# GpSimd subtracts the last contraction tile of a weight's low part

## The chip, the cores and the metric

The kernel runs on one core of one Trainium2 chip. The metric is the device time of one execution in microseconds (us), the median of several runs. Before the change it is 1791.72 us (three runs, 1791.2 to 1794.84).

## The reference

One decoder layer on a sequence of 256 tokens with 2048 channels, all in fp32. A conditioning vector `c` is turned into six vectors by a 2048 x 12288 matrix (`w_ada`): shift, scale and gate for each of two sub-layers. Then:

```
h = x * (1 + sc1) + sh1
proj = h @ w_in                      # 2048 x 13344: q, k, v of two mixers, z, b, a, two gates
y_a  = softmax attention, 8 heads of 128, relative-position bias (256 tokens are one block)
y_b  = gated DeltaNet, 16 heads of 128: short conv, l2 norm of q and k, chunked delta rule, gated RMS norm
y    = (sigmoid(gate_a) * (y_a @ w_proj_moba) + sigmoid(gate_b) * (y_b @ w_proj_gdn)) @ w_out
x    = layer_norm(alpha * x + g1 * y)
h    = x * (1 + sc2) + sh2
y    = (silu(gate) * up) @ w_ffn_out,  gate, up = split(h @ w_ffn_in)     # 2048 x 11264, 5632 x 2048
out  = layer_norm(alpha * x + g2 * y)
```

## The kernel before, in words

**Three products for one.** TensorE multiplies in fp32r, a rounded fp32. For accuracy each fp32 operand is split into a high part (the value rounded to fp32r) and a low part (the value minus its high part), and a product is taken as high x high + high x low + low x high. The activations are split once. Each weight is split as it comes in.

**One load of a weight.** `load_w` (L196) brings one block of a weight from HBM into a buffer `raw` of 128 partitions x 1024 elements at most; the block holds `kn` contraction tiles of 128 rows, `cn` columns each, side by side. `split_w` (L202) makes the parts: ScalarE copies `raw` to `hi` (L206), which rounds it, and VectorE subtracts, `lo = raw - hi` (L207). `raw`, `hi` and `lo` have four buffers each. The loads are issued by SP (SyncE) in one queue, in order; the load that reuses a buffer waits until the readers of the old contents are done.

**The list of steps.** `step` (L250) appends to a list a pair: the load with its split, and the matmuls that use it. `run(3)` walks the list and calls load and split up to three steps ahead of the matmuls. A scheduler then orders each engine's instructions by this order and its own estimate of when each can start; on the chip each engine works through its own queue in order, and semaphores tie the engines together. GpSimd's queue holds, besides a little arithmetic, the issue of some 70 small DMAs (`sdma`), which store and reload intermediate results through HBM.

**Who uses the loads.** `ws_mm` (L271) is the common form: for each contraction tile `i` of the load and each of two column halves it issues high x high (L276), high x low (L277) and low x high (L278), 256 columns each, so a load of four tiles takes 24 matmuls, and `lo` of tile `i` is first read by the third matmul of that tile. `xs_unit` (L309, matmuls L324 to L326) uses blocks of 512 columns and two tiles, or of 256 columns and four tiles in the last two column blocks of an output projection. `ws_wide` (L280) is for the feed-forward input weights.

**The stages in order.**

- The opening (to about 280 us). The activations become ready in five groups of contraction tiles, of 2, 3, 3, 4 and 4 tiles (`GROUPS`), because shift and scale are still being computed. For each group, `startup` goes over 20 column blocks of `w_in` (a load of `kn` = 2, 3 or 4 tiles each), and the products of a group are added into SBUF by VectorE (L434, `kq`, `v`, `qk`), one operand being TensorE's accumulator bank in PSUM. Between them VectorE works through the ada sums (L231): each multiplies a 128x1024 block of `w_ada` with the conditioning vector and sums along the row. Their blocks go to a ring of eight buffers of their own here (`r`).
- The token mixer (to about 945 us). Units of four loads with four tiles each (`ws_unit`): the remaining attention queries and keys, both gates, both branch projections. Between them, loads of two tiles (attention values, z). A background list (`bg`, advanced by `tick` after every load) interleaves the attention and DeltaNet work, and the rest of the ada sums, whose blocks now share the four `raw` buffers (`raw_a`).
- The output projection (945 to 1035 us), the start of the feed-forward part, the feed-forward input (1095 to 1535 us), the feed-forward output (to 1778 us), and the final norm, in which GpSimd does one of the eight column pieces (L1174, L1175) and VectorE the others.

Of the kernel before, what the change touches and what calls it, by code (L numbers as in the profile page):

```python
# [10 lines left out]
F32 = mybir.dt.float32  # L11
F32R = mybir.dt.float32r
AF = mybir.ActivationFunctionType
OP = mybir.AluOpType
# [78 lines left out]
def layer(ctx, tc, a, out):  # L93
    nc = tc.nc
    v_, s_, g_, t_, dma = nc.vector, nc.scalar, nc.gpsimd, nc.tensor, nc.sync
# [100 lines left out]
    def load_w(w, k0, kn, c0, cn):  # L196
        raw = wp.tile([P, 1024], F32, tag="raw", name="raw", bufs=4)
        v = raw[:, :kn * cn].rearrange("p (k n) -> p k n", n=cn)
        dma.dma_start(raw[:, :kn * cn], w.tile(k0, kn, c0, cn))
        return v  # L200

    def split_w(raw, kn, cn):  # L202
        hi = wp.tile([P, 1024], F32R, tag="hi", name="hi", bufs=4)
        lo = wp.tile([P, 1024], F32R, tag="lo", name="lo", bufs=4)
        hi, lo = [t[:, :kn * cn].rearrange("p (k n) -> p k n", n=cn) for t in (hi, lo)]
        s_.copy(hi, raw)  # L206
        v_.tensor_tensor(lo, raw, hi.bitcast(F32), op=OP.subtract)  # L207
        return hi, lo

    def split(hi, lo, src, scale=None):  # L210
# [37 lines left out]
    prog = []  # L248

    def step(w, k0, kn, c0, cn, post):  # L250
        prog.append((lambda: split_w(load_w(w, k0, kn, c0, cn), kn, cn), post))

    def do(fn):
        prog.append((None, fn))
# [41 lines left out]
    def ws_part(box, ops, w, c0, k0, k1, kt, fin):  # L296
        for k in range(k0, k1, 4):
            def post(hi, lo, k=k):
                if k == 0:
                    box.append(mm())  # L300
                ws_mm(box[0], ops, hi, lo, k, 4, k == 0, k == kt - 4)
                if k == kt - 4:
                    fin(pairs_of(box[0]))
                tick()

            step(w, k, 4, c0, 256, post)

    def xs_unit(ops, w, c0, kt, fin, cn=512):
        kn = 1024 // cn  # L309
        box = []  # L310
        for k0 in range(0, kt, kn):
            def post(hi, lo, k0=k0):
                if k0 == 0:
                    box.extend([mm()[:, :cn], mm()[:, :cn]])
                last = k0 + kn == kt
                order = [(i, h) for i in range(kn) for h in range(2)]
                if last:
                    order = [(i, h) for h in range(2) for i in range(kn)]
                for i, h in order:
                    k = k0 + i  # L320
                    start, stop = k == 0, k == kt - 1
                    xh = ops[0][k][:, h * P:(h + 1) * P]
                    xl = ops[1][k][:, h * P:(h + 1) * P]
                    t_.matmul(box[h], xh, hi[:, i, :], start=start, stop=False)  # L324
                    t_.matmul(box[h], xh, lo[:, i, :], start=False, stop=False)  # L325
                    t_.matmul(box[h], xl, hi[:, i, :], start=False, stop=stop)  # L326
                if last:
                    fin(box)
                tick()

            step(w, k0, kn, c0, cn, post)
# [90 lines left out]
    def startup(n):  # L422
        k0, kn = GROUPS[n]
        more = n + 1 < len(GROUPS)
        if more:
            do(lambda: load_x(*GROUPS[n + 1]))
        for i, (c0, dst) in enumerate(jobs):
            def post(hi, lo, i=i, dst=dst):
                ps = mm()
                ws_mm(ps, h_ops, hi, lo, k0, kn, True, True)  # L430
                if n == 0:
                    s_.copy(dst, pairs_of(ps))
                else:
                    v_.tensor_tensor(dst, dst, pairs_of(ps), op=OP.add)  # L434
                ada_to(ada_goal(n, i))
                if more and i == 14:
                    prep(*GROUPS[n + 1])
                if not more and i == len(jobs) - 1:
                    ada_to(4 * KT + 2 * EARLY)

            step(w_in, k0, kn, c0, 256, post)
# [769 lines left out]
```

## Time and profile before

| | before |
|---|---|
| median of runs | 1791.72 us |
| profiled execution | 1797.65 us |
| its span, first to last instruction | 1795.9 us |
| mean granted TensorE clock | 0.979 |
| busy: TensorE / VectorE / ScalarE / GpSimd | 1695.2 / 1262.3 / 814.7 / 51.5 us |
| VectorE's weight subtractions (L207) | 572, 673.4 us |

The profile is one execution; times in the rows are counted from the start of its span. "PE" is TensorE's matmuls, "PEld" its weight loads, DVE is VectorE, ACT ScalarE, POOL GpSimd, SP SyncE; a "q" behind an engine's name is its queue of waits and DMA issues. A busy share is an average over stages with different limits. A row `A <- B` in the answer on waits says that A stood until B was done.

### The profile page before, as it was taken

To read this page: it belongs to the slowest core of one execution; us is meant where nothing else is said; L and a number is where in the kernel's file an instruction comes from. 1 tells how busy PE (TensorE), PEld (TensorE's weight loads), DVE (VectorE), ACT (ScalarE), POOL (GpSimd) and SP (SyncE) were. 2 spreads that over 40 slices of the span, in tenths; PEclk is the share of its full clock that TensorE was granted. 3 is DMA by queue.
4 is the path that set the end of the run, shared out by engine and by line. 5 is a ranking of instruction groups with operands and counts; after the bars stand their busy time and mean duration, and the time that the engine had idled before them with its cause. 6 is when DMAs were issued, how large, how long until landed. Compare 5 with 4: busy or idle time off the path is not lost.

```text
span 1795.9 us, 28491 instructions
## 1 busy us (share of the span) xinstructions
PE 1695.2 (94%) x11149; PEld 1543.4 (86%) x11149; DVE 1262.3 (70%) x1878; ACT 814.7 (45%) x1117; POOL 51.5 (3%) x71
## 2 busy tenths in 40 slices
PE   2999999999999999899999989999999999999995
PEld 1888999879999788899998889888888888888895
DVE  5899998888956687667775668666666655455454
ACT  2544445668433445335344434544444444333332
POOL 1000000111010001000000000000000000000001
PEclk9999999999989999899999989999999999999998
DMA  9999986656676577776886647777777765755652
GB/s 330 365 333 347 324 293 210 209 185 196 196 258 227 186 239 237 268 252 192 285 263 237 195 127 246 252 250 236 235 238 242 237 202 193 258 191 189 198 186 82
DMA packets 120584, 421.58 MB, mean 235 GB/s; under 512 B 13729, under 2 KB 14689, under 8 KB 119937
## 3 DMA queue, kind: packets, MB, share of 16 engines
q1 hardware_dynamic: 115344, 402.20, 66.6%
q0 software_dynamic: 5104, 17.55, 3.5%
q8 instruction: 88, 1.44, 0.3%
q14 instruction: 48, 0.39, 0.1%
HBM read 412.27 MB, written 7.42 MB: 234 GB/s over the span
## 4 chain that ended last, share of the span: by engine, by line
PE 44%; issue 15%; DMA 6%; DVE 5%; ACT 1%; POOL 0%; POOLq 0%; DVEq 0%; ACTq 0%
PE mm L283 16%; PE mm L287 8%; PE mm L277 3%; PE mm L278 3%; PE mm L276 3%; DMA raw_a<-in_w_ada 3%; DVE lo L207 3%; PE mm L325 2%; PE mm L326 2%; PE mm L324 2%; DMA raw<-in_w_in 2%; DMA raw<-in_w_proj_gdn 1%; PE ps L658 1%; ACT hi L206 1%; DVE Ub L633 0%
## 5 line engine op out<-in xcount | busy, mean ns | idle before, releaser
L206 ACT CAST hi<-raw 128x1024 fp32r<-128x1024 f32 (+2 forms) x572 | 582.6, 1020 | 776.9 <-PE mm L326 202.5
L207 DVE TENSOR_TENSOR lo<-raw,hi 128x1024 fp32r<-128x1024 f32 (+2 forms) x572 | 673.4, 1183 | 281.7 <-ACT hi L206 279.7
L278 PE MATMUL mm<-s,lo 128*128 128x256 f32 x1280 | 363.7, 285 | 9.5 <-DVE lo L207 8.7
L276 PE MATMUL mm<-s,hi 128*128 128x256 f32 x1280 | 365.3, 286 | 5.4 <-ACT hi L206 5.4
L277 PE MATMUL mm<-s,hi 128*128 128x256 f32 x1280 | 359.7, 281 | 0.0
L283 PE MATMUL mm<-h,hi 128*128 128x512 f32 x1280 | 319.0, 391 | 0.0
L283 PEld LDWEIGHTS mm<-h,hi 128*128 128x128 f32 x1280 | 228.8, 188 | 39.4
L278 PEld LDWEIGHTS mm<-s,lo 128*128 128x128 f32 x1280 | 242.5, 190 | 17.0 <-DVE lo L207 15.2
L276 PEld LDWEIGHTS mm<-s,hi 128*128 128x128 f32 x1280 | 243.3, 190 | 9.3 <-ACT hi L206 6.7
L277 PEld LDWEIGHTS mm<-s,hi 128*128 128x128 f32 x1280 | 243.0, 190 | 0.3
L287 PEld LDWEIGHTS mm<-h,lo 128*128 128x128 f32 x1280 | 171.1, 188 | 13.2
L287 PE MATMUL mm<-h,lo 128*128 128x256 f32 x1280 | 174.1, 278 | 0.0
L324 PE MATMUL mm<-hi,ach 128*128 128x512 f32 (+1 forms) x440 | 152.6, 347 | 0.0
L325 PE MATMUL mm<-lo,ach 128*128 128x512 f32 (+1 forms) x440 | 152.5, 347 | 0.0
L326 PE MATMUL mm<-hi,acl 128*128 128x512 f32 (+1 forms) x440 | 152.5, 347 | 0.0
L231 DVE CUSTOM_DVE_ANT_0 raw_a<-raw_a,cb,cols 128x1024 f32<-128x1024 f32 x56 | 71.8, 1282 | 75.9 <-DMA raw_a<-in_w_ada 75.9
L231 DVE CUSTOM_DVE_ANT_0 raw_a<-raw_a,cb,ada_half 128x1024 f32<-128x1024 f32 x56 | 71.8, 1282 | 65.0 <-DMA raw_a<-in_w_ada 64.9
L324 PEld LDWEIGHTS mm<-hi,ach 128*128 128x128 f32 x440 | 83.3, 189 | 10.4
L326 PEld LDWEIGHTS mm<-hi,acl 128*128 128x128 f32 x440 | 83.3, 189 | 10.3
L325 PEld LDWEIGHTS mm<-lo,ach 128*128 128x128 f32 x440 | 83.3, 189 | 10.2
L325 PE MATMUL mm<-lo,s 128*128 128x512 f32 x192 | 77.1, 402 | 2.7 <-DVE lo L207 2.7
L324 PE MATMUL mm<-hi,s 128*128 128x512 f32 x192 | 78.7, 410 | 0.0
(285 smaller groups left out, 2297.5 us busy)
## 6 DMA issues: line engine op xcount, KB each, us to landing
raw<-in_w_ffn_in SPq DMA_DIRECT2D x176, 512.0 KB, 4.3
raw<-in_w_in SPq DMA_DIRECT2D x168, 512.0 KB, 4.3
raw_a<-in_w_ada SPq DMA_DIRECT2D x112, 512.0 KB, 4.6
raw<-in_w_ffn_out SPq DMA_DIRECT2D x88, 512.0 KB, 4.2
r<-in_w_ada SPq DMA_DIRECT2D x80, 512.0 KB, 6.2
raw<-in_w_proj_gdn SPq DMA_DIRECT2D x32, 512.0 KB, 4.4
raw<-in_w_out SPq DMA_DIRECT2D x32, 512.0 KB, 3.6
raw<-in_w_in SPq DMA_DIRECT2D x40, 384.0 KB, 5.4
```

Of the source, the lines that this page charges most:

```text
L206: s_.copy(hi, raw)
L207: v_.tensor_tensor(lo, raw, hi.bitcast(F32), op=OP.subtract)
L231: v_.tensor_tensor_reduce(out=raw, in0=raw, in1=cb[:, 1024 * half:1024 * half + 1024], scale=1.0, scalar=h if half else cols[:, col:col + ...
L276: t_.matmul(o, hi[:, i, c], ah, start=(first and i == 0 and t == 0), stop=False)
L277: t_.matmul(o, hi[:, i, c], al, start=False, stop=False)
L278: t_.matmul(o, lo[:, i, c], ah, start=False, stop=(last and i == kn - 1 and t == 1))
L283: t_.matmul(box[t].rearrange("p (u i) -> p u i", u=2), hi[:, i, t * P:(t + 1) * P], both[k0 + i], start=(first and i == 0), stop=False)
L287: t_.matmul(box[t][:, :S], lo[:, i, t * P:(t + 1) * P], both[k0 + i][:, 0, :], start=False, stop=(last and i == kn - 1))
L324: t_.matmul(box[h], xh, hi[:, i, :], start=start, stop=False)
L325: t_.matmul(box[h], xh, lo[:, i, :], start=False, stop=False)
L326: t_.matmul(box[h], xl, hi[:, i, :], start=False, stop=stop)
L658: t_.matmul(ps[:lt.shape[1], n, :], lt, rt, start=True, stop=True)
```

## The change

Where a load has more than two contraction tiles and isn't one of the feed-forward input weights, VectorE subtracts all tiles but the last, and GpSimd subtracts the last one, always 128x256 elements. Both write into the same `lo` buffer. Which loads these are follows from `kn`: 80 in the opening (the groups of 3 and 4 tiles), 128 in the token mixer (all `ws_unit` loads), and, since those blocks also have four tiles, 8 in the last two column blocks of `w_out` and 22 in the last two of `w_ffn_out`; 238 in all. ScalarE's copy and the matmuls stay as they are.

```diff
-    def split_w(raw, kn, cn):
+    def split_w(raw, kn, cn, shared):
         hi = wp.tile([P, 1024], F32R, tag="hi", name="hi", bufs=4)
         lo = wp.tile([P, 1024], F32R, tag="lo", name="lo", bufs=4)
         hi, lo = [t[:, :kn * cn].rearrange("p (k n) -> p k n", n=cn) for t in (hi, lo)]
         s_.copy(hi, raw)
-        v_.tensor_tensor(lo, raw, hi.bitcast(F32), op=OP.subtract)
+        last = kn - 1 if shared else kn
+        v_.tensor_tensor(lo[:, :last], raw[:, :last], hi[:, :last].bitcast(F32), op=OP.subtract)
+        if shared:
+            g_.tensor_tensor(lo[:, last:], raw[:, last:], hi[:, last:].bitcast(F32), op=OP.subtract)
         return hi, lo
...
     def step(w, k0, kn, c0, cn, post):
-        prog.append((lambda: split_w(load_w(w, k0, kn, c0, cn), kn, cn), post))
+        prog.append((lambda: split_w(load_w(w, k0, kn, c0, cn), kn, cn, kn > 2 and w.name != "in_w_ffn_in"), post))
```

## Rows read from the trace of the kernel before

**Rows 1.** The page: busy us (share of the span) and instructions by engine.
```profile
PE 1695.2 (94%) x11149; PEld 1543.4 (86%) x11149; DVE 1262.3 (70%) x1878; ACT 814.7 (45%) x1117; POOL 51.5 (3%) x71
```

**Rows 2.** The page: 40 slices of the span, busy tenths of VectorE, GB/s moved.
```profile
DVE  5899998888956687667775668666666655455454
...
GB/s 330 365 333 347 324 293 210 209 185 196 196 258 227 186 239 237 268 252 192 285 263 237 195 127 246 252 250 236 235 238 242 237 202 193 258 191 189 198 186 82
```

**Rows 3.** Busy by stage: stretch, us, busy (count) by engine, clock, DMA, GB/s.
```profile
50.00:200.00 150.00, 141.66 (x1122) 132.60 (x1123) 143.92 (x217) 67.68 (x97) 0.00 (x0) 1.00 0.95 344
245.00:280.00 35.00, 35.00 (x299) 35.00 (x299) 35.00 (x52) 18.42 (x24) 1.07 (x2) 1.00 0.74 248
320.00:945.00 625.00, 595.52 (x4191) 553.92 (x4190) 463.24 (x810) 302.53 (x473) 36.08 (x49) 0.96 0.70 228
1095.00:1780.00 685.00, 681.33 (x3866) 597.90 (x3864) 410.16 (x480) 303.42 (x369) 1.07 (x2) 1.00 0.66 217
```

**Rows 4.** Waits from 50 to 245 us: us in total, times, longest us.
```profile
ACT hi L206 <- DMA raw<-in_w_in: 58.8, 33, 3.3
PEld mm L278 <- DVE lo L207: 13.7, 25, 1.7
```

**Rows 5.** Waits from 320 to 945 us, TensorE's and VectorE's.
```profile
PE ps L658 <- DVE z L667: 6.4, 3, 3.1
PE mm L278 <- DVE lo L207: 3.4, 6, 0.8
...
DVE kq L564 <- DMA rb<-rnd: 14.4, 5, 6.6
```

**Rows 6.** VectorE in order of time, 175 to 191 us: start, us, instruction.
```profile
176.75 1.22 DVE L207 TENSOR_TENSOR lo<-raw,hi 128x1024 fp32r<-128x1024 f32 x1
177.89 0.68 DVE L434 TENSOR_TENSOR kq<-kq,mm 128x512 f32<-128x512 f32 x1
...
188.71 1.22 DVE L207 TENSOR_TENSOR lo<-raw,hi 128x1024 fp32r<-128x1024 f32 x1
```

**Rows 7.** VectorE's instructions by shape: count, busy us, mean ns, idle before.
```profile
L207 DVE TENSOR_TENSOR lo<-raw,hi 128x1024 fp32r<-128x1024 f32 x512 | 622.1, 1221 | 274.6 <-ACT hi L206 272.8
...
L207 DVE TENSOR_TENSOR lo<-raw,hi 128x768 fp32r<-128x768 f32 x40 | 37.8, 951 | 0.7 <-ACT hi L206 0.6
...
L207 DVE TENSOR_TENSOR lo<-raw,hi 128x512 fp32r<-128x512 f32 x20 | 13.5, 688 | 6.4 <-ACT hi L206 6.3
```

**Rows 8.** Line L207 from 50 to 200 us: ns min/median/max, starts, shapes.
```profile
L207 DVE TENSOR_TENSOR lo<-raw,hi x63: 683/951/1222, 50.9 to 199.5; 128x768 fp32r<-128x768 f32 x40, 128x512 fp32r<-128x512 f32 x12, 128x1024 fp32r<-128x1024 f32 x11
```

**Rows 9.** Line L207 by stretch: us, VectorE busy (count), clock, DMA, GB/s.
```profile
200.00:280.00 80.00, 35.73 (x30) 1.00 0.84 292
```

**Rows 10.** VectorE and SP in order of time, 725 to 739 us.
```profile
728.26 0.33 SPq L199 DMA_DIRECT2D raw<-in_w_in  x1
...
733.74 1.23 DVE L207 TENSOR_TENSOR lo<-raw,hi 128x1024 fp32r<-128x1024 f32 x1 [0.69 <-ACT hi L206]
...
734.99 0.33 SPq L199 DMA_DIRECT2D raw<-in_w_in  x1
```

**Rows 11.** VectorE's groups from 320 to 945 us: count, busy us, mean ns.
```profile
L231 DVE CUSTOM_DVE_ANT_0 raw_a<-raw_a,cb,cols 128x1024 f32<-128x1024 f32 x38 | 48.7, 1281 | 41.2 <-DMA raw_a<-in_w_ada 41.2
```

**Rows 12.** Lines L1174 and L1175, the tail: ns min/median/max, first and last start.
```profile
L1174 DVE TENSOR_TENSOR r<-r,b x7: 680/683/691, 1780.7 to 1787.4; 128x512 f32<-128x512 f32 x7
L1174 POOL TENSOR_TENSOR r<-r,b x1: 4761/4761/4761, 1785.7 to 1785.7; 128x512 f32<-128x512 f32 x1
...
L1175 DVE TENSOR_TENSOR r<-r,b x7: 680/682/693, 1781.4 to 1788.6; 128x512 f32<-128x512 f32 x7
L1175 POOL TENSOR_TENSOR r<-r,b x1: 1261/1261/1261, 1790.5 to 1790.5; 128x512 f32<-128x512 f32 x1
```

**Rows 13.** GpSimd's groups from 320 to 945 us: count, busy us, mean ns, idle before.
```profile
L645 POOL DMA_DIRECT2D TT<-ubd x4 | 3.6, 896 | 62.1 <-PE ps L658 50.6 <-DMA ubd<-mt 11.5
...
L617 POOL DMA_DIRECT2D Mb<-mbd x2 | 2.2, 1112 | 14.2 <-issue 8.2 <-DMA mbd<-ma 6.0
```

## The prediction, made before the result was known

> **What bounds the kernel now.** I read the page's busy shares first, then its 40 slices, then the busy times by stage, then the waits of the stages that are not full, and last single rounds in order of time.
>
> TensorE is busy for 94% of the span, VectorE for 70%, GpSimd for 3% [rows 1]. That names TensorE, but the slices show VectorE at 8 or 9 tenths through the opening, slices 2 to 6 [rows 2], so the stage table decides [rows 3]. The unit for it is one TensorE matmul of 256 columns: 299 of them fill 35.00 us in 245 to 280 us, where TensorE never pauses, so 0.117 us each. In 50 to 200 us, 1122 matmuls need 131.3 us of 150: 18.7 us are lost there, with VectorE busy 143.92 us (96%) and the DMA engines at 0.95. In 320 to 945 us, the mixer, TensorE is busy 595.52 of 625 us, idle for 29.5, and its granted clock is 0.96 on average, so some stretches ran at the lower of its two levels and a little more is lost. In 1095 to 1780 us, the feed-forward part, TensorE is busy 681.33 of 685 us. A change to VectorE can therefore gain only in the opening and in the mixer. The 22 shared loads of the last projection lie where TensorE is full already, and the 8 of the projection before it are too few to count: nothing for both.
>
> The waits say what the losses hang on. In 50 to 245 us the weight load of a low part waits for VectorE's subtraction for 13.7 us in 25 waits, and ScalarE waits for a weight's landing for 58.8 us in 33 [rows 4]. In 320 to 945 us TensorE waits for VectorE's z (6.4 us in 3 waits) and lo (3.4 in 6) [rows 5], and with the smaller rows of that answer 22 of its waits are VectorE's.
>
> One round of the opening shows its pace: subtraction, accumulation of a partial product (kq), one ada sum, next subtraction. From 176.75 to 188.71 us there are four such rounds without a pause on VectorE, 2.99 us each [rows 6]. TensorE needs 24 x 0.117 = 2.81 us for a load's 24 matmuls. VectorE sets the pace, by 0.18 us.
>
> **What is removed.** 238 loads have their VectorE subtraction cut by one tile: 80 in the opening (40 of three tiles, 40 of four), 128 in the mixer's four-tile units, 30 in the two projections. By shape the subtraction takes 1221 ns for 1024 elements a partition, 951 for 768 and 688 for 512 [rows 7]: 0.27 us is saved for a four-tile load, 0.263 for a three-tile one.
>
> **Opening.** Between 50 and 200 us stand 63 subtractions: 40 of 768, 11 of 1024, and 12 of 512 that stay as they are [rows 8]; 30 more follow to 280 us [rows 9], where TensorE takes over as the bound. VectorE is relieved of 40 x 0.263 + 11 x 0.27 = 13.5 us to 200 us. TensorE could take 18.7. But the transfers have to follow: 344 GB/s over 150 us, at the 365 GB/s of the fastest slice [rows 2], is 141.4 us, so they give 8.6 us at most. I take 8, from 0 (the transfers are at their limit already) to 13.5.
>
> **Mixer.** 128 x 0.27 = 34.6 us leave VectorE, whose 463.24 busy us in 625 leave room already. What comes back is the lateness of results for which TensorE stands: 22 waits shortened by 0.27 each are 5.9 us. A second source is the circle of the raw buffers, which weight loads share with ada weights here: a load issued at 728.26 is subtracted at 733.74, and its buffer is reloaded at 734.99 [rows 10], 6.73 us for two loads, 3.37 each where TensorE needs 2.81. If the GpSimd part is ready before the shorter VectorE part, the circle loses 0.27, 0.13 per load; with the 76 ada sums of this stage (38 first halves and as many second ones) [rows 11] that would be 10 us, mostly hidden by the loads made ahead. I take 4 for both sources together, bounds 0 and 15; below nothing it goes only by rivals A and C.
>
> **What is added.** 238 GpSimd subtractions of 128x256. The trace has two of 128x512: 4761 ns, VectorE busy beside it, and 1261 ns alone [rows 12]. Half of 1261, 0.63 us, is the floor, 4.76 the ceiling, if the first one's surroundings were the rule. VectorE's shapes show a fixed cost of 2 x 688 - 1221 = 155 ns; with the same on GpSimd it is (1261 - 155)/2 + 155, 0.71 us. I take that, by the row that ran alone: 169 us on an engine that is busy for 51.5. It is hidden by the order of the matmuls: the last tile's low part is read 18 matmuls (12 for three tiles) after the first one's, 2.1 or 1.4 us later. Without that cover, as when a read of the first tile waits for both writers, it still ends before VectorE's 0.95, unless something holds it up. The reload of a raw buffer now waits for both engines, and the next load on SP's queue stands behind it; by the same 0.71 against 0.95 that wait is free.
>
> **The first call and the tail.** The longer of the two could hold a first-use cost of 3.5 us. It then moves to the opening, where the 1.4 us of cover and VectorE's 0.69 leave 4.76 - 2.1 = 2.7 us; I take 2, less a bit of lead. In the tail GpSimd's last add ends at 1790.5 + 1.26 = 1791.8 us and VectorE's last at 1788.6 + 0.69 = 1789.3 [rows 12], and the last store waits for the later one. A warm GpSimd that starts at 1785.7 is done by 1788.2, and 2.5 us go. Bounds: 0 and -2.5 for the tail, 0 and +2.7 for the first use.
>
> The Trainium skill (GPSIMD Engine Reference, section 2.1) says that the first call of a freshly loaded kernel pays about 6 us that no instruction shows; by that the +2 would be +5 or so, and no row here tells it from the reading under rival A.
>
> **Sum.** -8 - 4 + 2 - 2.5 = -12.5, against the profiled execution's own 1797.65 us (span 1795.9 and 1.75 around it): 1785. That execution is 5.9 us above the median of the runs, 1791.72, so I carry the difference over: 1780 us, rounded.
>
> **Rivals.**
>
> *A, the two engines get in each other's way.* The 4761 ns can be read otherwise: GpSimd stood still while VectorE ran its adds up to 1789.3, and took 1.1 us more to 1790.4. VectorE's adds beside it kept their 680 to 693 ns [rows 12]. Nothing in the trace shows a warm GpSimd subtraction beside VectorE. If each holds the other off, the opening's round has only the 0.68 us of kq, whose one operand is an accumulator bank, for GpSimd's 0.71; what does not fall there delays VectorE by 0.03 to 0.71 us, less 0.27 saved: -0.24 to +0.44 per load. Halfway, 0.10 for the 81 shared loads to 280 us, is +8. In the mixer both start when the cast ends; the later one then ends 0.95 + 0.71 after it, 0.44 later than now, and the circle of raw buffers grows by 0.22 per load. 76 of them are 17 us, of which I let a third through: +6. Sum +14: 1806 us (1797 to 1818). It decides if GpSimd delays VectorE by more than 0.27 us per load on average. For it: both start on one event. Against: the undisturbed adds.
>
> The Trainium skill has this as a rule (SBUF — State Buffer, "Who interferes with whom"): a VectorE instruction with two SBUF inputs contends with a GpSimd one that reads SBUF, and the second to issue is blocked until the first is done. The 4761 ns row agrees and does not prove it.
>
> *B, a wash.* GpSimd gives way and runs beside kq, or the opening is held by its transfers anyway. The 58.8 us of landing waits speak for it; that VectorE never pauses in the rounds speaks against. The opening gives 2, the mixer 0 to 2, the tail nothing: 1789 us (1785 to 1795).
>
> *C, GpSimd's queue.* It runs in order, and in the mixer its DMA issues wait there: 11.5 us in two for a store to land before TT, 6.0 in one before Mb [rows 13]. A subtraction behind such a wait is 3 to 6 us late, more than the 2.1 of cover; the three loads made ahead, 8.4 us, cover most of the rest, and I count 1 us for each of 8 such places. In the other direction the issue of rb goes behind subtractions that wait for a cast, and VectorE, which already stands 14.4 us for rb [rows 5], stands 0.7 more for each of its 8. +13.6 less the opening's 8: 1797 us.
>
> **Chances and range.** Forecast 0.45, A 0.25, B 0.20, C 0.10. The forecast's own range is 1769 to 1787 (the opening gives 13 to 4, the mixer 9 to 1; all bounds at one end at once are not likely). A measurement of this kernel tells 0.2%, 3.6 us, from no change, so faster means under 1788.1 and slower over 1795.3. Faster: 0.45 x 0.93 + 0.20 x 0.35 + 0.02 of A and C = 0.51. Same: 0.03 + 0.10 + 0.05 = 0.18. Slower: 0.31, nearly all of it A and C. For 8 in 10 the range runs from 1771 to 1808, leaving out the best of the forecast and the worst of A.
>
> **What would show it.** Right: VectorE's part of a four-tile load at 0.95 us with ada sums still at 1.28; GpSimd at 0.6 to 0.8 us from the second one on; more matmuls in the first 200 us; the four-tile round at 2.81. Wrong: ada sums or subtractions on VectorE well beyond those, or gaps ahead of them (A); GpSimd subtractions of 1.5 us and more with VectorE's untouched (B); GpSimd waiting for a landing, and TensorE for a low part right behind it (C). The prediction falls if the first 280 us get no shorter.

## The result, and the profile after

The change makes the kernel slower: 1816.4 us (median of 4 runs, 1814.44 to 1816.72) against 1792.24 (4 runs, 1791.2 to 1794.84). The ratio is 1.0128 [1.0108, 1.0147], which is 23 us; the two medians lie 24.2 us apart. The forecast was 1780 with a range to 1808. The profiled execution of after took 1816.57 us, 18.9 more than that of before, at the same mean granted clock, 0.979. VectorE's subtraction L207 is now L208, GpSimd's new one is L210, and the lines behind `split_w` stand three lower than before.

The page of after, beside [rows 1]:
```profile
PE 1694.7 (93%) x11149; PEld 1542.1 (85%) x11149; DVE 1260.5 (69%) x1878; ACT 810.6 (45%) x1115; POOL 322.8 (18%) x309
```
TensorE's busy time is that of before. VectorE was relieved of 238 tiles and is busy for 1260.5 us where it was 1262.3: what was taken off it came back.

The opening and the mixer of after, columns as in [rows 3]; the second row is the mixer from its first weight load of L328 (the next fence but one) to the output projection:
```profile
50.00:200.00 150.00, 137.50 (x1082) 129.15 (x1082) 136.44 (x210) 65.75 (x95) 48.96 (x51) 0.99 0.93 332
314.30:960.90 646.60, 600.43 (x4219) 556.54 (x4217) 477.34 (x832) 302.29 (x474) 170.29 (x168) 0.96 0.69 224
```
From 50 to 200 us after does 40 matmuls fewer than before, and 332 GB/s are moved where it was 344. The feed-forward part is unchanged: TensorE is busy for 681.15 us of 685. For the stage borders I take the first weight load of L325 (now L328) in each stage. Low parts as the operand, before:
```profile
L325 PEld LDWEIGHTS mm<-lo,s x192: 186/188/337, 311.5 to 702.3; 128*128 128x128 f32 x192
L325 PEld LDWEIGHTS mm<-lo,mh x160: 187/188/192, 942.8 to 1030.7; 128*128 128x128 f32 x160
```
and after:
```profile
L328 PEld LDWEIGHTS mm<-lo,s x192: 186/188/337, 314.3 to 716.0; 128*128 128x128 f32 x192
L328 PEld LDWEIGHTS mm<-lo,mh x160: 187/188/192, 960.9 to 1048.9; 128*128 128x128 f32 x160
```
Of the 18.9 us the opening has 2.8, the mixer 15.3 (646.6 against 942.8 - 311.5 = 631.3), the rest 0.8.

That execution of before was a long one, 5.4 us above the median. There is a second trace to compare with: tail_vector, an experiment below, differs from before in the last piece of the final norm alone and took 1793.23 us in its profiled execution. Its mixer, from its first weight load of L325:
```profile
312.20:938.40 626.20, 596.02 (x4219) 553.42 (x4217) 470.16 (x830) 305.26 (x476) 35.51 (x48) 0.97 0.72 231
```
Against this one after is 23.3 us longer, of which the opening has 2.1, the mixer 20.4 and the rest 0.8.

The waits of after from 50 to 245 us [rows 4]:
```profile
ACT hi L206 <- DMA raw<-in_w_in: 66.7, 42, 4.2
PEld mm L281 <- DVE lo L208: 17.5, 26, 2.2
```
and from 320 to 961 us [rows 5]:
```profile
DVE kq L567 <- DMA rb<-rnd: 14.7, 5, 7.4
...
PE ps L661 <- DVE z L670: 7.9, 2, 5.1
PE mm L281 <- DVE lo L208: 5.9, 10, 1.3
```
All but the wait for rb have grown by a tenth or more. No row of TensorE's in either stretch names GpSimd's part as what it waited for.

VectorE and GpSimd by shape [rows 7], whole span; the first column of times is the busy sum, the second the mean in ns:
```profile
L210 POOL TENSOR_TENSOR lo<-raw,hi 128x256 fp32r<-128x256 f32 x238 | 271.4, 1143 | 747.4 <-ACT hi L206 640.7 <-DMA raw<-in_w_in 65.3 <-PE mm L280 9.4
L208 DVE TENSOR_TENSOR lo<-raw,hi 128x768 fp32r<-128x768 f32 x198 | 207.1, 1049 | 76.9 <-ACT hi L206 75.3 <-PE ps L661 1.2
L234 DVE CUSTOM_DVE_ANT_0 raw_a<-raw_a,cb,cols 128x1024 f32<-128x1024 f32 x56 | 77.1, 1376 | 86.5 <-DMA raw_a<-in_w_ada 85.9 <-POOL lo L210 0.6
```
GpSimd's subtraction takes 1143 ns in the mean, not 710. VectorE's of 768 takes 1049 where the same shape took 951. The ada sums, which read a block and the conditioning vector `cb`, went from 1281 to 1376, and in the mixer alone [rows 11] to:
```profile
L234 DVE CUSTOM_DVE_ANT_0 raw_a<-raw_a,cb,cols 128x1024 f32<-128x1024 f32 x38 | 54.0, 1420 | 48.5 <-DMA raw_a<-in_w_ada 47.9 <-POOL lo L210 0.6
```

Line L208 from 50 to 200 us [rows 8]:
```profile
L208 DVE TENSOR_TENSOR lo<-raw,hi x61: 676/689/1489, 49.5 to 198.2; 128x512 fp32r<-128x512 f32 x52, 128x768 fp32r<-128x768 f32 x9
```
The shapes are the shorter ones, and there are 61 of them where there were 63. From 200 to 280 us [rows 9] there are 29 where there were 30.

Rounds of the opening in order of time, all engines, with the wait of an instruction in brackets [rows 6]:
```profile
180.62 0.74 POOL L210 TENSOR_TENSOR lo<-raw,hi 128x256 fp32r<-128x256 f32 x1 [1.83 <-PE mm L281]
180.67 0.68 DVE L437 TENSOR_TENSOR kq<-kq,mm 128x512 f32<-128x512 f32 x1
...
188.24 0.77 POOL L210 TENSOR_TENSOR lo<-raw,hi 128x256 fp32r<-128x256 f32 x1 [1.79 <-ACT hi L206]
188.33 1.49 DVE L208 TENSOR_TENSOR lo<-raw,hi 128x768 fp32r<-128x768 f32 x1
...
190.34 1.27 DVE L234 CUSTOM_DVE_ANT_0 r<-r,cb,ada_half 128x1024 f32<-128x1024 f32 x1
190.77 1.45 POOL L210 TENSOR_TENSOR lo<-raw,hi 128x256 fp32r<-128x256 f32 x1 [1.76 <-ACT hi L206]
191.55 1.48 DVE L208 TENSOR_TENSOR lo<-raw,hi 128x768 fp32r<-128x768 f32 x1
```
The three pairs show what the two engines do to each other. At 180.62 GpSimd runs beside kq, whose one operand is an accumulator bank: 0.74 us, and neither is longer. At 188.24 both subtract: VectorE's lasts 1.49, 0.54 more than the 0.951 of [rows 7], and 0.68 us of GpSimd's subtraction fall into it. At 190.77 VectorE is in an ada sum, which keeps its 1.27; GpSimd's subtraction starts beside it and takes 1.45, and VectorE's next one, which starts before GpSimd's has ended, takes 1.48.

The circle of the raw buffers in the mixer [rows 10], all engines:
```profile
733.49 1.05 ACT L206 CAST hi<-raw 128x1024 fp32r<-128x1024 f32 x1 [1.95 <-DVE ada_half L234]
734.57 0.96 DVE L208 TENSOR_TENSOR lo<-raw,hi 128x768 fp32r<-128x768 f32 x1 [0.25 <-ACT hi L206]
734.61 1.51 POOL L210 TENSOR_TENSOR lo<-raw,hi 128x256 fp32r<-128x256 f32 x1 [2.25 <-ACT hi L206]
735.57 1.64 DVE L234 CUSTOM_DVE_ANT_0 raw_a<-raw_a,cb,ada_half 128x1024 f32<-128x1024 f32 x1
736.15 0.33 SPq L199 DMA_DIRECT2D raw<-in_w_in  x1
```
Both subtractions start when the cast ends at 734.54. VectorE's is first and ends at 735.53; GpSimd's ends at 736.12, and only then, at 736.15, is the buffer loaded again. The ada sum that fell on the same time took 1.64 us. SP's queue shows how often GpSimd was the last reader. After, 320 to 960 us, then 50 to 245 us (us in total, times, longest):
```profile
SPq L199 <- DVE lo L208: 241.3, 112, 10.2
SPq L199 <- POOL lo L210: 34.6, 40, 5.8
...
SPq L199 <- POOL lo L210: 3.5, 7, 0.6
```
Forty times in the mixer, seven times in the opening. Before, the first of these rows was 214.2 us in 97, and there was no second. The other buffers that GpSimd now holds count too: ScalarE's cast waited for GpSimd's subtraction for 20.4 us in 11 waits of the whole span.

The tail [rows 12]:
```profile
L1177 POOL TENSOR_TENSOR r<-r,b x1: 4777/4777/4777, 1804.5 to 1804.5; 128x512 f32<-128x512 f32 x1
L1178 DVE TENSOR_TENSOR r<-r,b x7: 680/683/693, 1800.2 to 1807.5; 128x512 f32<-128x512 f32 x7
L1178 POOL TENSOR_TENSOR r<-r,b x1: 1262/1262/1262, 1809.4 to 1809.4; 128x512 f32<-128x512 f32 x1
```
The 4.8 us add is still there, although GpSimd had done 238 subtractions by then. It ends at 1809.3, 1.1 us after VectorE's last add (1807.5 + 0.68 = 1808.2). This is rival A's reading: most of the 4.8 us are a wait for VectorE.

### The profile page after: what moved, and what is told of

Read it like the earlier page. It is cut to its first block, busy times and chain, and to the rows that moved or that the text cites. A ratio compares the mean times of both kernels' runs of the same rounds, so it can differ in the third digit from the quotient of the medians.

```text
span 1814.7 us, 29260 instructions
## 1 busy us (share of the span) xinstructions
PE 1694.7 (93%) x11149; PEld 1542.1 (85%) x11149; DVE 1260.5 (69%) x1878; ACT 810.6 (45%) x1115; POOL 322.8 (18%) x309
## 4 chain that ended last, share of the span: by engine, by line
PE 70%; DVE 12%; DMA 10%; issue 4%; ACT 2%; POOL 1%; SPq 0%; POOLq 0%; DVEq 0%; ACTq 0%
PE mm L286 16%; PE mm L290 8%; PE mm L281 7%; PE mm L329 7%; PE mm L328 7%; PE mm L327 7%; PE mm L280 7%; PE mm L279 7%; DVE lo L208 5%; DMA raw_a<-in_w_ada 4%; DMA raw<-in_w_in 2%; DMA raw<-in_w_proj_gdn 1%; DMA r<-in_w_ada 1%; DVE tm L634 1%; DVE r L234 1%
## 5 line engine op out<-in xcount | busy, mean ns | idle before, releaser
L208 DVE TENSOR_TENSOR lo<-raw,hi 128x1024 fp32r<-128x1024 f32 (+2 forms) x572 | 632.5, 1110 | 292.1 <-ACT hi L206 288.5
L210 POOL TENSOR_TENSOR lo<-raw,hi 128x256 fp32r<-128x256 f32 x238 | 271.4, 1143 | 747.4 <-ACT hi L206 640.7
L281 PEld LDWEIGHTS mm<-s,lo 128*128 128x128 f32 x1280 | 243.5, 190 | 22.1 <-DVE lo L208 20.4
L328 PE MATMUL mm<-lo,ach 128*128 128x512 f32 (+1 forms) x440 | 152.5, 347 | 0.0
L234 DVE CUSTOM_DVE_ANT_0 raw_a<-raw_a,cb,cols 128x1024 f32<-128x1024 f32 x56 | 77.1, 1376 | 86.5 <-DMA raw_a<-in_w_ada 85.9
L234 DVE CUSTOM_DVE_ANT_0 raw_a<-raw_a,cb,ada_half 128x1024 f32<-128x1024 f32 x56 | 76.0, 1357 | 58.0 <-DMA raw_a<-in_w_ada 57.9
L328 PEld LDWEIGHTS mm<-lo,ach 128*128 128x128 f32 x440 | 83.3, 189 | 10.2
```

Source lines behind the costliest of these rows:

```text
L208: v_.tensor_tensor(lo[:, :last], raw[:, :last], hi[:, :last].bitcast(F32), op=OP.subtract)
L210: g_.tensor_tensor(lo[:, last:], raw[:, last:], hi[:, last:].bitcast(F32), op=OP.subtract)
L234: v_.tensor_tensor_reduce(out=raw, in0=raw, in1=cb[:, 1024 * half:1024 * half + 1024], scale=1.0, scalar=h if half else cols[:, col:col + ...
L281: t_.matmul(o, lo[:, i, c], ah, start=False, stop=(last and i == kn - 1 and t == 1))
```

## The experiments

The theory after the result: the engines hold each other off while both read two operands (rival A), and, a part of its own, the raw buffer comes back later because its last reader is later. Its rivals: TensorE waits for GpSimd's part; GpSimd's queue is late with its DMA issues; the scheduler put TensorE's, ScalarE's and SP's work into another order. The differences below are (ratio - 1) x 1793 us. The kernels `relief_...` and `acc_...` leave the low part of the last tile out: the matmuls read that of the tile before it a second time.

| kernel | ratio | 95% | us |
|---|---|---|---|
| after | 1.0128 | 1.0108 to 1.0147 | +23.0 |
| relief_only | 0.9958 | 0.9941 to 0.9974 | -7.5 |
| relief_208 | 0.9949 | 0.993 to 0.9969 | -9.1 |
| relief_onecol | 1.0008 | 0.9996 to 1.002 | +1.4 |
| opening_only | 1.0002 | 0.9992 to 1.0011 | +0.4 |
| mixer_only | 1.014 | 1.0123 to 1.0157 | +25.1 |
| acc_onecol | 0.9988 | 0.9974 to 1.0002 | -2.2 |
| acc_write | 0.9997 | 0.9983 to 1.001 | -0.5 |
| acc_copy | 0.9987 | 0.9977 to 0.9998 | -2.3 |
| acc_hold | 1.0036 | 1.002 to 1.0052 | +6.5 |
| acc_subhi | 1.0051 | 1.0034 to 1.0068 | +9.1 |
| acc_sub128 | 1.006 | 1.0038 to 1.0082 | +10.8 |
| acc_sub | 1.0134 | 1.0121 to 1.0147 | +24.0 |
| cast_on_pool | 1.0082 | 1.0063 to 1.01 | +14.7 |
| tail_vector | 1.0002 | 0.9988 to 1.0016 | +0.4 |

**relief_only: VectorE's relief without GpSimd's work.**
```diff
-        if shared:
-            g_.tensor_tensor(lo[:, last:], raw[:, last:], ...)
...
-                t_.matmul(o, lo[:, i, c], ah, ...
+                t_.matmul(o, lo[:, i - (kn > 2 and i == kn - 1), c], ah, ...
```


> VectorE's subtraction is cut by one tile in the same 238 loads, and GpSimd does nothing; the low part of the last tile is left out, and the matmuls read the low part of the tile before it a second time. Same count of matmuls. Theory P (the two engines hold each other off at SBUF; the relief by itself is sound): 8 to 15 us faster than before, about 1780 us, ada sums back at 1.28 us. Theory R (the relief is worth nothing where it stands, since transfers or TensorE set the pace; the loss is from GpSimd's work in any case): within 4 us of before. Theory O (the new order of the queues that the scheduler makes costs the time, whoever does the work): slower than before by 10 us or more.

Measured: -7.5 us, just under the 8 to 15 of theory P. Every instruction of TensorE, ScalarE and SP stands in the same order as in after, and this kernel is faster than before: the order is not what makes after slower. TensorE's and ScalarE's order is not that of before, though, so the gain is that of the relief and the new order together. **relief_208** is the same for the opening's and the mixer's 208 loads alone (`shared = kn > 2 and w.name in ("in_w_in", "in_w_proj_moba", "in_w_proj_gdn")`):

> relief_only restricted to the 208 loads of the opening and the mixer; the last tile's low part is left out. If the 30 loads of the projections are worth nothing, as I costed them: as relief_only, 5 to 9 us faster than before, and then the 5 us to acc_onecol are GpSimd's: its own DMA issues standing behind subtractions that wait for a cast, and buffers given back later. If it comes out as acc_onecol, within 2 us of it, GpSimd's queue costs nothing.

Measured: -9.1 us. The two intervals overlap: the 30 loads of the projections are worth nothing that these runs can tell.

**opening_only and mixer_only: the change in one stage.**
```diff
-    prog.append((lambda: split_w(load_w(...), kn, cn, kn > 2 and w.name != "in_w_ffn_in"), post))
+    shared = kn > 2 and not mixing                  # opening_only
+    shared = kn > 2 and bool(mixing) and w.name in ("in_w_in", "in_w_proj_moba", "in_w_proj_gdn")   # mixer_only
+    prog.append((lambda: split_w(load_w(...), kn, cn, shared), post))
```


> The change in the 80 loads of the opening alone. Theory P: VectorE never idles there and its round has only kq beside which GpSimd runs free, so about a quarter of the loss, +4 to +8 us over before. Theory Q: GpSimd's queue holds almost no DMA issue before 280 us, so nothing is lost, 0 or a few us faster.

> The change in the mixer's 128 loads alone, the opening and the two projections as before. Theory P and theory Q both: +12 to +18 us over before, since the trace after loses about 15 us there; with opening_only it adds up to the whole (+23). If the two add up to clearly less, the 30 loads of the projections or the order of the queues count as well.

Measured: 0.4 us with an interval over nothing for the opening's 80 loads, and +25.1 for the mixer's 128, more than the 12 to 18 of both theories. In the whole time the mixer pays for all of it. The trace of opening_only says more of the opening itself; its row from 50 to 200 us and its first weight load of the mixer:
```profile
50.00:200.00 150.00, 136.82 (x1080) 128.00 (x1081) 139.35 (x209) 65.69 (x95) 54.74 (x51) 1.00 0.93 331
```
```profile
L330 PEld LDWEIGHTS mm<-lo,s x192: 186/188/337, 316.6 to 701.4; 128*128 128x128 f32 x192
```
There are 1080 matmuls where before has 1122, and the mixer starts at 316.6, 5.1 us later than in before and 4.4 later than in tail_vector. VectorE's subtractions of 768 up to 280 us take 1038 ns in the mean there, for 951 in before: the two engines hold each other up in the opening too. The mixer of this execution, whose loads are not shared, then takes 621.9 us, 4.3 less than tail_vector's; 3.0 of them are TensorE's busy time, at a granted clock of 0.98 for 0.97. Why it makes up for the opening stays open.

**relief_onecol: GpSimd kept in the chain, with nearly no reading.** It subtracts one column of the last tile into a scratch tile of its own.
```diff
+            px = wp.tile([P, 1, 1], F32, tag="px", name="px", bufs=1)
+            g_.tensor_tensor(px, raw[:, last:, :1], hi[:, last:, :1].bitcast(F32), op=OP.subtract)
```


> As relief_only, but GpSimd subtracts one single column of the last tile into a scratch tile, so that its queue, its waits for the cast and the hold on the raw buffer are those of the change, without its reading time; the low part of the last tile is left out as there. Theory P: like relief_only, within 4 us, since 128x1 takes the shared way to SBUF for next to nothing. Theory Q (GpSimd's queue in order and the added waits are the cost: subtractions behind DMA issues, rb's issues behind subtractions, raw buffers held): slower than relief_only by 10 us or more, with VectorE's instructions at their plain lengths.

Measured: +1.4 us, of which a part is not what the run was for. In the last projection, where nothing else differs, TensorE is full in both kernels and did fewer matmuls in 100 us. From the output projection to the end of the span relief_onecol takes 859.7 us (1798.6 - 938.9), relief_only 852.6 (1786.3 - 933.7): 7.1 us, in one trace each, that are not GpSimd's queue. Without them the run would stand at -5.7, near relief_only. From 1600 to 1700 us, columns as in [rows 3], before and then relief_onecol:
```profile
1600.00:1700.00 100.00, 100.00 (x443) 82.81 (x442) 48.59 (x43) 38.57 (x37) 0.00 (x0) 1.00 0.61 196
```
```profile
1600.00:1700.00 100.00, 100.00 (x430) 80.53 (x429) 47.52 (x42) 37.15 (x37) 0.00 (x0) 1.00 0.58 190
```
At the same granted clock a matmul took 3% more. The new four-byte tile shifts the addresses of others by 32 bytes, and after and relief_only, which have no such tile, did 443 in this stretch as before did; that the shift is the reason was not tried further. The rest of the family therefore writes into a spare buffer of an existing ring (`tag="acc"`), for the 208 loads, and no matmul reads it:

**acc_onecol, acc_write, acc_copy, acc_sub.**
```diff
+            px = wp.tile([P, 1, 512], F32, tag="acc", name="px", bufs=2)
+            g_.tensor_tensor(px[:, :, :1], raw[:, last:, :1], hi[:, last:, :1]...)         # acc_onecol, acc_write
+            g_.memset(px[:, :, 1:512], 0.0)                                                # acc_write, as well
+            g_.tensor_copy(px[:, :, :256], hi[:, last:]...)                                # acc_copy
+            g_.tensor_tensor(px[:, :, :256], raw[:, last:], hi[:, last:]...)               # acc_sub
```


> As relief_onecol, for the 208 loads of the opening and the mixer, and with the single column written into a buffer that the kernel has anyway, so that no other tile changes its place (in relief_onecol a new tile moved the others, and TensorE's matmuls of the last projection took 233 ns in place of 227). The last tile's low part is left out. Theory P: as relief_only, 5 to 9 us faster than before. Theory Q (queue, waits, order): at least 4 us slower than relief_only, that is within 3 us of before.

> As acc_onecol, and after the single column GpSimd sets 511 columns of the spare buffer to zero: about as busy as with the subtraction, but reading nothing. Theory P with reading as the shared resource: within 4 us of acc_onecol, VectorE's instructions at their plain lengths. If any work of GpSimd in SBUF holds VectorE up: 10 us or more slower than acc_onecol.

> As acc_sub, but GpSimd copies 128x256 from the high part, one operand read in place of two; same order. Theory P, if reading is what counts: VectorE is held up about half as long per load, so 5 to 12 us slower than acc_onecol. If only instructions with two operands hold each other up: like acc_onecol within 3 us, with ada sums at 1.28.

> As acc_onecol, but GpSimd subtracts the whole 128x256 into the spare buffer; TensorE, ScalarE and SP have the same instructions in the same order as in acc_onecol, VectorE but for one pair. No matmul reads GpSimd's result; the last tile's low part is left out. Theory P: the whole loss shows here, 15 to 25 us slower than acc_onecol, with VectorE's subtractions of 768 at 1.0 us and more and its ada sums at 1.35. Theory L (the matmuls wait for GpSimd's late part): like acc_onecol within 4 us.

Measured: -2.2, -0.5, -2.3 and +24.0 us. By its own expectation acc_onecol is theory Q's case, within 3 us of before: GpSimd in the chain costs something with hardly any reading. acc_sub is as slow as after although no matmul waits for its result, so a late part is not the cause. Writing 511 columns costs nothing that can be measured. Copying 256 comes out as one column does, but the copy doesn't hold `raw`, and the one column does, so this doesn't show that its reading is free. The whole loss over one column, 26.2 us, comes with the subtraction of the whole tile.

**acc_subhi, acc_sub128, acc_hold: reading, size and holding apart.** acc_subhi subtracts hi from hi: two operands, but `raw` isn't held. acc_sub128 does half the columns. acc_hold does one column after the cast, two memsets of 511 columns, then one column again: `raw` and `hi` are held for about 1 us more, and hardly read.
```diff
+            g_.tensor_tensor(px[:, :, :256], hi[:, last:]..., hi[:, last:]...)             # acc_subhi
+            g_.tensor_tensor(px[:, :, :128], raw[:, last:, :128], hi[:, last:, :128]...)   # acc_sub128
+            g_.tensor_tensor(px[:, :, :1], ...); g_.memset(px[:, :, 1:512], 0.0)           # acc_hold
+            g_.memset(px[:, :, 1:512], 1.0); g_.tensor_tensor(px[:, :, 511:512], ...)      # acc_hold
```


> As acc_sub, in the same order on all engines, but GpSimd subtracts the high part from itself, so that it reads two operands and no longer holds the raw buffer; the last tile's low part is left out. If the later reload of raw buffers carries the loss in the mixer: at least 8 us faster than acc_sub. If it is VectorE's delayed instructions alone: as acc_sub within 4 us, about +24 us over before.

> As acc_sub with half of the columns, 128x128, same order on TensorE, ScalarE and SP; the last tile's low part is left out. If the loss goes with the time that GpSimd's reading takes from VectorE: about half, +9 to +14 us over before, with VectorE's busy time in the mixer midway between acc_onecol and acc_sub. If it is a matter of meeting at all: +20 us and more.

> As acc_onecol, in the same order on the other engines, but GpSimd reads one column after the cast, sets the spare buffer twice (about 1.05 us, nothing read), and reads one column again, so that it gives the raw and high buffers back more than a microsecond after the cast, as in acc_sub, and VectorE is not held up. The last tile's low part is left out. If the raw buffers carry the mixer's loss: 8 to 16 us slower than acc_onecol, with VectorE's instructions at their plain lengths. If it takes VectorE's delay: within 4 us of acc_onecol.

Measured: +9.1, +10.8 and +6.5 us. Over one column, two-operand reading that holds only `hi` costs 11.3, holding with hardly any reading 8.7, and both together 26.2; half the columns 13.0, half of it. The 8.7 rest on the medians, and GpSimd's queue is busier in acc_hold as well; that SP's loads wait for GpSimd is in the traces, of acc_onecol and then acc_hold, 320 to 960 us:
```profile
SPq L199 <- POOL px L211: 14.8, 7, 5.8
```
```profile
SPq L199 <- POOL px L211: 47.9, 57, 3.9
```
A busier queue by itself is not the loss: in the mixer GpSimd is busy for 273 us in acc_hold and for 171 in acc_sub, which is 17.5 us slower. The stage rows of the mixer (columns as in [rows 3]) show VectorE's part. Before:
```profile
311.50:942.80 631.30, 601.82 (x4219) 558.96 (x4218) 468.41 (x828) 304.67 (x477) 35.54 (x48) 0.96 0.70 228
```
relief_208, acc_onecol and acc_hold:
```profile
308.90:931.20 622.30, 592.88 (x4219) 551.94 (x4218) 439.78 (x829) 302.11 (x475) 35.54 (x48) 0.98 0.71 232
```
```profile
306.40:938.40 632.00, 595.00 (x4219) 553.61 (x4218) 440.47 (x830) 302.53 (x474) 105.91 (x168) 0.97 0.70 228
```
```profile
306.30:939.80 633.50, 597.56 (x4219) 556.16 (x4218) 441.90 (x830) 301.93 (x475) 273.07 (x526) 0.96 0.70 228
```
acc_subhi and acc_sub:
```profile
312.50:945.00 632.50, 592.75 (x4219) 550.39 (x4217) 464.47 (x827) 302.52 (x474) 157.93 (x168) 0.98 0.70 228
```
```profile
314.50:964.30 649.80, 598.54 (x4219) 554.76 (x4218) 474.87 (x830) 302.55 (x474) 170.96 (x168) 0.97 0.69 222
```
VectorE's busy time, the third pair, is where reading shows: 468 before, 440 to 442 with the relief, also in acc_hold, and 464 and 475 where GpSimd reads two operands. TensorE's idle time (stretch less busy) is what it costs: 29.5 before (30.2 in tail_vector), 29.4 in relief_208, 37.0, 35.9, 39.8 and 51.3 in the others in this order; after has 46.2. These are single executions: acc_hold's was the fastest of its 12, and its row doesn't show the 8.7. The busy time of TensorE for the same 4219 matmuls goes with the granted clock, 0.96 to 0.98.

The lengths say who slows whom. VectorE's 768 subtraction in acc_onecol, acc_copy and acc_sub:
```profile
L208 DVE TENSOR_TENSOR lo<-raw,hi 128x768 fp32r<-128x768 f32 x168 | 159.8, 954 | 45.1 <-ACT hi L206 44.6
```
```profile
L208 DVE TENSOR_TENSOR lo<-raw,hi 128x768 fp32r<-128x768 f32 x168 | 163.8, 977 | 37.9 <-ACT hi L206 37.5
```
```profile
L208 DVE TENSOR_TENSOR lo<-raw,hi 128x768 fp32r<-128x768 f32 x168 | 171.8, 1026 | 33.5 <-ACT hi L206 30.8 <-PE mm L284 2.0
```
and GpSimd's own, ns min/median/max, in acc_onecol, acc_copy, acc_sub128 and acc_sub:
```profile
L211 POOL TENSOR_TENSOR px<-raw,hi x208: 181/463/1989, 72.6 to 928.1; 128x1 f32<-128x1 f32 x104
```
```profile
L211 POOL COPY px<-hi x208: 397/634/2912, 73.2 to 924.3; 128x256 f32<-128x256 f32 x104
```
```profile
L211 POOL TENSOR_TENSOR px<-raw,hi x208: 443/822/2237, 72.3 to 940.8; 128x128 f32<-128x128 f32 x104
```
```profile
L211 POOL TENSOR_TENSOR px<-raw,hi x208: 716/1030/3544, 74.1 to 954.0; 128x256 f32<-128x256 f32 x104
```
The Trainium skill (SBUF — State Buffer, "Who interferes with whom") has the two engines share a pair of ports with an exclusive lock. The traces agree: VectorE's subtraction goes from 954 to 1026 ns beside GpSimd's, and every kind of GpSimd's reads here is longer in the median than at its shortest, the single column too (463 for 181), while acc_write's memset, which reads nothing, keeps to 514 to 544 ns. The copy lengthened VectorE's by 23 ns. That it reads one operand and not two need not be the reason: acc_sub128 reads two, is about as short by itself (443 ns for 397), and VectorE's subtraction takes 980 ns beside it for 977 beside the copy. VectorE's ada sums tell the two apart a little, 1322 ns for 1301, where [rows 11] has 1281. A one-operand instruction of 0.7 us was not tried.

**cast_on_pool: an attempt at a better version.** GpSimd casts the last tile, with one operand, and VectorE subtracts all of it.
```diff
-        s_.copy(hi, raw)
+        s_.copy(hi[:, :last], raw[:, :last])
+        if shared:
+            g_.tensor_copy(hi[:, last:], raw[:, last:])
-        v_.tensor_tensor(lo[:, :last], ...)
+        v_.tensor_tensor(lo, raw, hi.bitcast(F32), op=OP.subtract)
```


> A version that could beat both: GpSimd takes one-operand work only. In the 208 loads of opening and mixer ScalarE casts all tiles but the last, GpSimd casts the last, and VectorE subtracts the whole block as before. The cast is 0.27 us shorter and ready earlier; acc_copy shows 0.63 us for such a GpSimd copy in the median and VectorE lengthened by 1 to 2%. Expected 0 to -5 us against before; if GpSimd's copy comes late behind VectorE's reading (acc_copy has some of 2.9 us), the whole subtraction waits for it: +5 to +15 us.

Measured: +14.7 us. VectorE has no relief, and from 320 to 950 us 21 of its subtractions wait for GpSimd's cast, 12.9 us in all and 3.0 at the longest.

**tail_vector: the tail's eighth piece on VectorE too,** in the kernel before.
```diff
-            e = g_ if (n == 3 and h == 1) else v_
+            e = v_
```


> The kernel before with the last column piece of the final norm on VectorE in place of GpSimd. If the 4.76 us of GpSimd's first add are waiting for VectorE (theory P), VectorE ends 1.2 us later than before, at about 1790.5 on the clock of the profiled execution, and the last store starts there and not at 1791.8: 1.3 us faster, too little for the ratio to tell; the trace's tail tells it.

Measured: +0.4 us with an interval over nothing, though in its trace the last store's issue ends 11.4 us after the norm's scale is made, and 12.5 in before's: 1.1 us at the most.

The kernels that beat before leave the last tile's low part out; none that computes it does.

## Why the prediction was wrong

It forecast -12.5 us and +23 came. Its rival A named the mechanism and some three fifths of the size, with a range (to 1818) that holds the result.

- **"What is added", the step that failed.** It took 0.71 us for GpSimd's subtraction "by the row that ran alone", and called it hidden by the matmul order. Its shortest of the 238 is 0.716 us; in its place it is 1143 ns in the mean and up to 2.8 us, and VectorE's work beside it grows too. [rows 12] held two durations of one instruction, and the 4761 ns was the one taken beside VectorE. In the kernel the whole subtraction costs 26.2 us over one column of it (acc_sub over acc_onecol).
- **"By the same 0.71 against 0.95 that wait is free."** With both starting at the cast's end GpSimd's is the later one, 40 times in the mixer. Holding the buffers about 1 us longer, with two more GpSimd instructions that read hardly anything and a busier queue, costs 8.7 us (acc_hold over acc_onecol; the interval of the difference is about 4 to either side).
- **"Hidden by the order of the matmuls."** That held: TensorE waited for no late part, and acc_sub, whose result nobody reads, is as slow. The cover was counted for the result; the buffers and VectorE had none.
- **Opening, -8, and mixer, -4.** The relief, with its new order, gives -9.1, so the sum of -12 is right in kind. How it divides depends on the trace of before: against its own profiled execution relief_208 has 2.6 of it in the opening (308.9 against 311.5) and 9.0 in the mixer (622.3 against 631.3), against tail_vector's, which is nearer to the median, 3.3 and 3.9. The opening then gave less than half of its 8, and the mixer's 4 came out, but not by the way that was forecast: TensorE's idle time there went from 30.2 us to 29.4, where the 22 lateness waits alone were to give 5.9, and the rest is TensorE's busy time, at a granted clock of 0.98 for 0.97. As far as one pair of traces tells, that the size fits is luck.
- **The first call and the tail, +2 and -2.5.** Both rest on a first use that isn't there: the first of the 238 subtractions starts at 72.93 us, 0.08 after its cast has ended, and the 4777 ns came again from a GpSimd that had done 238 of them. The tail gave 1.1 us at the most (tail_vector).
- **Rival A, +14.** Its ground was that "both start on one event", and that holds in the mixer only. VectorE's subtractions of 768, from 50 to 280 us and in the mixer:
```profile
L208 DVE TENSOR_TENSOR lo<-raw,hi 128x768 fp32r<-128x768 f32 x38 | 39.2, 1031 | 0.5 <-ACT hi L206 0.5
...
L208 DVE TENSOR_TENSOR lo<-raw,hi 128x768 fp32r<-128x768 f32 x120 | 127.1, 1064 | 31.4 <-ACT hi L206 30.0 <-PE ps L661 1.2
```
In the opening they wait 0.5 us in all for the cast: VectorE comes to them late, and GpSimd starts ahead of it. In the mixer they wait 30.0 us, and start with GpSimd. Both get longer, though, 1031 and 1064 ns for 951. A's +8 for the opening is right in kind: the stage ends 5.1 us later in opening_only and 2.8 in after, though the total of opening_only shows none of it. For the mixer A had 17 us and "let a third through"; mixer_only measured +25.1.
- **Rival C, +5.3 over before.** acc_onecol is 6.9 slower than relief_208, with about 4 to either side, and relief_onecol without its 7.1 would be 1.8 slower than relief_only. GpSimd in the chain, with hardly any reading, may be worth that much; whether it is its queue is not shown. The wait for rb, C's named place, did not grow (14.7 for 14.4), and the issues of TT and Mb wait no more than in [rows 13]:
```profile
L648 POOL DMA_DIRECT2D TT<-ubd x4 | 3.6, 902 | 8.6 <-DMA ubd<-mt 8.2 <-PE ps L661 0.4
L620 POOL DMA_DIRECT2D Mb<-mbd x2 | 2.2, 1104 | 11.5 <-issue 7.1 <-PE psS L794 4.3
```
- **Signs.** "The prediction falls if the first 280 us get no shorter": the opening ended 2.8 us later. "Ada sums or subtractions on VectorE well beyond those (A)": 1376 and 1049.

In medians, then, acc_sub, which stands for after without its 30 projection loads: -9.1 for the relief, +6.9 for GpSimd being in the chain at all, +8.7 for holding, +11.3 for two-operand reading, and 6.2 that appear when both come together (with 5 to either side, hardly told from nothing). These are steps from kernel to kernel and no clean prices: the one column already holds `raw` (SP's loads wait for it for 14.8 us in 7 waits) and waits beside VectorE, and the reading of acc_subhi does not hold it. What the 6.9 consist of stays open, and so does how the 11.3 divide between the blocked VectorE and the longer GpSimd.

## What to carry to other kernels

An idle engine is not a free one: before work goes to GpSimd beside a busy VectorE, look for a row in which both ran, and price the work by that row and not by the one alone. Count what the new reader holds as well as what waits for its result; a second reader of a load buffer delays the next load whenever it ends last. Here the split cost most where both engines wait for one event (the mixer, 128 loads, +25.1 us) and less where VectorE comes late (the opening, 80 loads, 5 us of the stage and none of the total); that the common event makes the difference was not tried by itself.

## What the runs showed that was not expected

- An instruction of GpSimd can be reported at 4.8 us where the same shape takes 1.26 with VectorE done: by all signs the wait for VectorE stands inside it. A long first call in a trace is no proof of a first-use cost.
- Even a single column that GpSimd reads takes 463 ns in the median for 181 at the shortest, and 256 columns subtracted from themselves cost 11.4 us more than 256 copied, though both hold only `hi`. The copy has one operand and is also shorter (397 ns at its shortest for 602); which of the two counts is not told apart.
- With a four-byte tile more in SBUF a full TensorE did 430 matmuls in 100 us for 443 at the same granted clock, and by one trace each the run lost 7.1 us that had nothing to do with its question. A variant that adds a tile is best compared in a stage that it should not change.
